# A depthwise convolution regrouped in PSUM, an expert decode on paired elements, and a gather ring of four

## The chip, the cores and the metric

The kernel runs on one core of a Trainium2 chip. The metric is the device time of one execution in microseconds (us). TensorE (PE) multiplies matrices, VectorE (DVE), ScalarE (ACT) and GpSimd (POOL) do elementwise work, and SyncE (SP) issues most of the DMAs. Each engine executes its own instructions in the order in which the program holds them, and waits on semaphores for the others.

## The reference, cut to what matters

Three parts of a long chain of layers matter here.

```python
# layer A: a causal depthwise convolution with 31 taps over 1536 channels, then LayerNorm and SiLU
h = a * sigmoid(gl)
h = conv(h, conv_w) + conv_b               # 12 tiles of 128 channels, 512 positions
y_mix = silu(layer_norm(h, g, b))          # then times silu(gate), then @ w_out

# peer_ffn, routing: per token and head the best 16 of 16 x 16 pair sums of two key lists
v1, i1 = top_k(s[:, :, 0], 16); v2, i2 = top_k(s[:, :, 1], 16)
top_s, pos = top_k(v1[..., :, None] + v2[..., None, :], 16)
idx = (i1 * 128 + i2) at pos; g = softmax(top_s)

# peer_ffn, experts: 16384 experts, 128 of them (8 heads x 16) chosen for each of 512 tokens
a = einsum('thkd,td->thk', u[idx], x); w = gelu(a) * g
out = einsum('thk,thkd->td', w, v[idx])
```

## The kernel before

Activations lie transposed, features on partitions and 512 tokens along the free axis. Float32 products are made of three matmuls (lines 164 to 166): each operand is split into a high part (a cast on ACT, `whi`, line 158) and a low part (a subtraction, `wlo`, line 159, on DVE or POOL by the argument `lo`).

The program is written stage by stage. A scheduler then orders the instructions of each engine by its own timeline, and tile pools with a fixed number of buffers bound how far it can run ahead: the next user of a buffer waits until its last reader is done.

**Layer A (`layer_a`, the first 400 us).** DVE makes eleven of the twelve convolution tiles: 31 multiply-adds (line 602, `cacc`) for each, a step of one tile followed by a step of its neighbour in the group `CGR`. The groups are (0,1), (3,4), (5,6), (7,8,9), (10,11). Two accumulators of a group lie in two PSUM banks; the third of (7,8,9), tile 9, lies in SBUF (tag `cva`). Tile 2 is made by ACT and POOL. Meanwhile PE makes the keys, values and attention of the memory (`mem_kv`, `mem_attn`, whose low parts `ak`, `av` and maxima `mmx` are made on DVE) and the gates. When the convolution is done, statistics are made (`cst` on PE, a chain on POOL), and broadcast as `Mb` and `Rb` in PSUM. Then for each tile: subtract the mean (line 607, DVE), multiply by `Rb` (four tiles on DVE, line 614; eight on POOL, line 616, from the SBUF copy `Rs`), scale and tanh on ACT, two products on DVE (lines 621 and 623), and the split into `y..h` and `y..l` (low parts of odd tiles on POOL, of even ones on DVE, line 187). The output projection on PE takes the y tiles in order, with weights split on ACT and DVE.

**Routing (`route`, to about 2010 us).** For tokens 384 to 511 (block t = 3) the 128 chosen experts of each token are fetched as rows: `gathered` issues an indirect DMA on POOL (line 1189; 128 rows of 8 KB, a u row and a v row) into the tile `grow`, DVE makes the dot product (line 1192) and adds the weighted v row to `pacc` (line 1199). `grow` has two buffers: gather n is issued when the addition of gather n - 2 is done. For the other 384 tokens all experts are computed densely. PE makes `u_tile` (24 matmuls of 384 columns each); 103 of the 128 tiles are spilled to DRAM (`a_spill`). `decode` turns positions into expert numbers on DVE by comparing with `tabs` (a table of 3 x 16 starts, copied out to 128 columns) and adding up steps; `dw` holds the steps copied out to 2048 columns by ACT. `gate_tiles` makes one-hot tiles on DVE (`oh`, `og`) which PE multiplies (`gp`, line 1319) into a table of gates, written to DRAM.

**Experts (`experts`, about 2010 to 2652 us).** For each of 128 expert tiles: load `vraw` (four buffers), split it (`vhi` on ACT, `vlo` on DVE), load the spilled `as` (four buffers) or make a fresh u tile (`pa`, every fifth, 25 in all), multiply by the gates `G`, split (`wh`, `wl`), and 18 matmuls of 512 columns into six PSUM banks (`po`). The rest of the 128 gathers lies between.

Of the kernel before, what the change touches and what calls it, by code (L numbers as in the profile page):

```python
# [17 lines left out]
OP = mybir.AluOpType  # L18
# [29 lines left out]
MLO = 6  # L48
CGR = (0, 1), (3, 4), (5, 6), (7, 8, 9), (10, 11)
NWARM = 8  # L50
# [8 lines left out]
class Body:  # L59
# [249 lines left out]
    def run(self):  # L309
        nc = self.nc  # L310
        self.vecs = self.const.tile([128, NVEC], F32, name="vecs")
        self.ident = self.const.tile([128, 128], F32, name="ident")
        self.ones = self.const.tile([128, 128], F32, name="ones")
        self.mhalf = self.const.tile([128, 8], F32, name="mhalf")
        nc.vector.memset(self.ones, 1.0)
        nc.vector.memset(self.mhalf, -0.5)
        self.hg_scale = self.const.tile([128, 1], F32, name="hg_scale")
        self.banks(alias=dict(o="s", Rb="cv", Mb="cv"), mm=(0, 1, 2), pt=(3, 4), s=(5,), cv=(6, 7))
        self.right = ExitStack()
        self.bk = self.right_pool("bk")  # L320
        if True:
            with self.phase("A", cva=1, slot=12, pcv=4, scr=2, asc=2, app=2, sq=2, accq=1, accs=1, back=4):
                with self.tc.tile_pool(name="mem", bufs=1) as self.mem:
                    self.layer_a()
            if self.stop == "a":
                self.right.close()
                return
            self.banks(mm=(0, 1), s=(2, 5), pt=(3, 4), o=(6, 7))
            with self.phase("B", slot=14, scr=4, asc=2, app=2, logit=3, alibi=2):
                self.layer_b()  # L330
        with self.right:
            self.banks(alias=dict(Rb="s", Mb="o"), mm=(0, 1, 2, 5), pt=(3, 4), s=(6,), o=(7,))
            with self.phase("B3", slot=24, scr=3, sq=2, accq=1, accs=1, back=2, raq=1, rsq=2, rtq=4, pp=3):
                self.b_out()
                self.ybp.close()
            if self.stop == "b":
                return
            self.banks(mm=(0, 1), s=(2, 5), pt=(3,), o=(4,), hx=(6, 7))
            self.early_c2 = ExitStack()
            self.c_mix()  # L340
            if self.stop == "c1":
                self.early_c2.close()
                return
            with self.early_c2, self.phase("C2", slot=24, scr=4, sq=2, accq=1):
                self.c_out()
            if self.stop == "c2":
                return
            self.pe = self.right_pool("pe")
            self.route_experts()
# [187 lines left out]
    def layer_a(self):  # L537
# [55 lines left out]
        for js in CGR:  # L593
            accs = [self.scr("cacc", tag="cva") if u == 2 else self.bank("cv", "cacc") for u in range(len(js))]
            for t in range(CK):
# [10 lines left out]
        for c in cs:  # L606
            nc.vector.tensor_tensor(c, c, Mb, op=OP.subtract)
        Rs = self.scr("Rs", tag="accs")
        nc.scalar.copy(Rs, Rb)
        for j in range(12):  # L610
            c = cs[j]
            n = self.scr("cn", tag=("asc", "app")[j % 2])
            if j % 3 == 0:
                nc.vector.tensor_tensor(n, c, Rb, op=OP.mult)
            else:
                nc.gpsimd.tensor_tensor(n, c, Rs, op=OP.mult)
            c = n
# [5 lines left out]
            nc.vector.scalar_tensor_tensor(y, c, 0.25, y, op0=OP.mult, op1=OP.mult)  # L623
            Y[4 + j] = self.split(y, f"y{j}", hi="s", lo="vg"[j % 2], x=2 <= j < 10, tag="slot" if j < 2 else "pcv")
        self.new_x()
# [558 lines left out]
    def gathered(self):  # L1184

        nc, n = self.nc, self.ng
        self.ng += 1
        gt = self.pe.tile([128, 2 * D], F32, name="grow", tag="grow", bufs=2)
        nc.gpsimd.indirect_dma_start(out=gt, out_offset=None, in_=self.i["peer_uv"],  # L1189
# [20 lines left out]
    def decode(self, vv, ii, tabs):  # L1210
# [11 lines left out]
        for h in range(8):  # L1222
            self.top16(c[:, h], ts[:, h], pos[:, h], 50)
        g = pool.tile([128, 8, 16], F32, name="g", tag="g", bufs=2)
        nc.vector.tensor_tensor(g, ts, ts[:, :, 0:1].to_broadcast([128, 8, 16]), op=OP.subtract)
# [7 lines left out]
        nc.vector.tensor_tensor(di[:, :, :, 1:16], ii[:, :, :, 1:16], ii[:, :, :, 0:15], op=OP.subtract)  # L1233
        dw = []
        for n in range(2):
            w = pool.tile([128, 16, 8, 16], BF16, name="dw", tag="dw", bufs=1)
            nc.scalar.copy(w, di[:, :, n].rearrange("p h r -> p r h").unsqueeze(3).to_broadcast([128, 16, 8, 16]))
            dw.append(w.rearrange("p r h k -> p r (h k)"))
        pf = pool.tile([128, 128], BF16, name="pf", tag="pf")
        nc.vector.tensor_copy(pf, pos.rearrange("p h k -> p (h k)"))  # L1240
        wide = [128, 16, 128]
        i1 = pool.tile([128, 128], F32, name="i1", tag="i1", bufs=2)
# [3 lines left out]
        def steps(src, n):  # L1246
            ge = pool.tile(wide, BF16, name="ge", tag="ge")
            nc.vector.tensor_tensor(ge, src.unsqueeze(1).to_broadcast(wide), tabs[:, n], op=OP.is_ge)
            return ge

        def total(ge, w, out):

            pr = pool.tile(wide, BF16, name="pr", tag="pr")
            nc.vector.tensor_tensor(pr, ge, w, op=OP.mult)
            n = 8
            while n:
                two = pr.rearrange("p (r two) x -> p r two x", two=2)
                o = out.unsqueeze(1) if n == 1 else pool.tile([128, n, 128], BF16, name="tree", tag=f"tree{n}")
                nc.vector.tensor_tensor(o, two[:, :, 0], two[:, :, 1], op=OP.add)
                pr, n = o, n // 2  # L1260

        ge = steps(pf, 0)
        total(ge, dw[0], i1)
        total(ge, tabs[:, 1], st)
        nc.vector.tensor_tensor(st, pf, st, op=OP.subtract)
# [3 lines left out]
    def route_tables(self):  # L1269
# [4 lines left out]
        nc.scalar.dma_start(starts, self.i["starts"])  # L1274
        tabs = pool.tile([128, 3, 16, 128], BF16, name="tabs")
        for n in range(3):
            nc.scalar.copy(tabs[:, n], starts[:, n].unsqueeze(2).to_broadcast([128, 16, 128]))
        rows = pool.tile([128, 128], F32, name="iota")
# [5 lines left out]
    def gate_tiles(self, t, ps):  # L1284
# [7 lines left out]
        nc.scalar.copy(g1, gs)  # L1292
        r = pool.tile([128, 128], F32, name="gr", tag="gr", bufs=2)
        nc.vector.tensor_tensor(r, gs, g1, op=OP.subtract)
# [30 lines left out]
    def experts(self):  # L1325
# [5 lines left out]
        for n in range(128):  # L1331
            e = n
            if n % 8 == 0:
                G = pool.tile([128, 24, 8, 16], F32, name="G", tag="G", bufs=2)
                nc.sync.dma_start(G.rearrange("p b n t -> p b (n t)"),
                                  self.gd[:, :, n * 16:n * 16 + 128].rearrange("b p c -> p b c"))
            vraw = pool.tile([128, D], F32, name="vraw", tag="vraw", bufs=4)
            nc.sync.dma_start(vraw, tab[e * 128:(e + 1) * 128, D:])
            vh, vl = self.split_w(vraw, "v", "v", 3, pool)
            vh, vl = (t.rearrange("p a b -> p (a b)") for t in (vh, vl))  # L1340
            if not self.fresh(e):
                a = pool.tile([128, ND], F32, name="as", tag="as", bufs=4)
                nc.sync.dma_start(a, self.ad[:, pre])
# [146 lines left out]
```

## Time and profile before

| | us |
|---|---|
| median of 3 runs (range) | 2709.32 (2707.19 to 2710.68) |
| the profiled execution, its own time | 2716.38 |
| span in the trace | 2714.4 |
| PE busy | 2621.4 (97% of the span) |
| DVE busy | 2077.2 (77%) |
| ACT busy / POOL busy | 1247.2 / 952.8 |

The busy time of PE is modelled: a matmul counts until its result is out, while the next one already streams. So the idle time of PE, the waits that end in it and the granted clock say more than the 97%. DVE, ACT and POOL rows overlap a little at their ends; the distance from start to start is what an instruction costs.

### The profile page before, as it was taken

The numbers are of one execution on the slowest core, as the hardware profiler recorded it, in microseconds if no ns is written. First come the engines' busy times: TensorE is split into PE (matmuls) and PEld (weight loads), VectorE is DVE, ScalarE is ACT, GpSimd is POOL, SyncE is SP. The second block draws the span as 40 slices with busy tenths as digits, with TensorE's granted clock in tenths as the row PEclk, the third lists the DMA queues.
The fourth block names the chain that finished last, engine by engine and source line by source line (L and its number), as shares of the span: only waits on it lengthen the run. The fifth ranks groups of instructions, "written<-read, shape, count | busy, mean of one in ns | idle before, by whom it ended". The sixth has DMA issues, their size and how long they took to land.

```text
span 2714.4 us, 40123 instructions
## 1 busy us (share of the span) xinstructions
PE 2621.4 (97%) x14581; PEld 2284.0 (84%) x14581; DVE 2077.2 (77%) x3926; ACT 1247.2 (46%) x2173; POOL 952.8 (35%) x654
## 2 busy tenths in 40 slices
PE   9989989999999999999999999999999999999998
PEld 7777879788889977788899999898898888888876
DVE  8999876695557678763679999888877877787765
ACT  4535554455545444333443555555543443343333
POOL 5965654332206555553431123223311121111201
PEclk9999999999999999999999999999999999999999
DMA  5233355223246311225733788788899899999952
GB/s 183 86 109 116 125 163 172 87 82 98 82 152 209 109 55 55 66 87 167 217 96 115 239 291 309 289 324 294 316 369 340 304 330 332 335 327 338 338 191 93
DMA packets 211958, 542.20 MB, mean 200 GB/s; under 512 B 18224, under 2 KB 105904, under 8 KB 192304
## 3 DMA queue, kind: packets, MB, share of 16 engines
q1 hardware_dynamic: 183488, 395.30, 44.3%
q0 software_dynamic: 18432, 134.23, 13.3%
q10 hardware_dynamic: 9840, 10.12, 1.2%
q8 instruction: 114, 1.87, 0.3%
q14 instruction: 84, 0.69, 0.1%
HBM read 468.99 MB, written 70.58 MB: 199 GB/s over the span
## 4 chain that ended last, share of the span: by engine, by line
PE 50%; DMA 14%; DVE 12%; issue 4%; ACT 2%; POOL 1%; SPq 0%; DVEq 0%; POOLq 0%; ACTq 0%
DMA grow<-peer_uv,pidx 9%; PE mm L164 9%; PE mm L165 9%; PE mm L166 8%; PE po L166 4%; PE po L164 4%; PE po L165 4%; DMA as<-a_spill 3%; PE out L164 2%; PE out L165 2%; PE out L166 2%; DVE pacc L1199 1%; DVE wlo L159 1%; DVE og L1312 1%; DVE hK L917 1%
## 5 line engine op out<-in xcount | busy, mean ns | idle before, releaser
L1189 POOL DMA_INDIRECT grow<-peer_uv,pidx x128 | 236.8, 1850 | 914.8 <-DVE pacc L1199 751.8
L158 ACT CAST whi<-wraw 128x1024 fp32r<-128x1024 f32 x360 | 377.6, 1050 | 383.9 <-PE mm L165 194.4
L159 POOL TENSOR_TENSOR wlo<-wraw,whi 128x1024 fp32r<-128x1024 f32 x157 | 380.7, 2427 | 419.6 <-ACT whi L158 360.9
L164 PE MATMUL po<-vhi,wh 128*128 128x512 f32 x768 | 297.1, 392 | 4.0 <-ACT wh L1351 4.0
L165 PE MATMUL po<-vlo,wh 128*128 128x512 f32 x768 | 299.0, 391 | 0.0
L159 DVE TENSOR_TENSOR wlo<-wraw,whi 128x1024 fp32r<-128x1024 f32 x203 | 260.1, 1283 | 48.2 <-ACT whi L158 45.4
L166 PE MATMUL po<-vhi,wl 128*128 128x512 f32 x768 | 273.6, 393 | 3.2 <-DVE wl L1352 3.2
L602 DVE SCALAR_TENSOR_TENSOR cacc<-h,vecs,cacc 128x512 f32<-128x512 f32 x319 | 240.0, 815 | 0.4
L1192 DVE SCALAR_TENSOR_TENSOR grow<-grow,hrow 128x1024 f32<-128x1024 f32 x128 | 156.6, 1223 | 101.2 <-DMA grow<-peer_uv,pidx 101.2
L166 PEld LDWEIGHTS po<-vhi,wl 128*128 128x128 f32 x768 | 143.9, 188 | 36.7 <-DVE wl L1352 6.6
L164 PEld LDWEIGHTS po<-vhi,wh 128*128 128x128 f32 x768 | 144.0, 188 | 34.2 <-ACT wh L1351 4.6
L165 PEld LDWEIGHTS po<-vlo,wh 128*128 128x128 f32 x768 | 144.3, 188 | 27.9
L159 DVE TENSOR_TENSOR vlo<-vraw,vhi 128x1024 fp32r<-128x1024 f32 x128 | 156.4, 1222 | 11.7 <-ACT vhi L158 11.6
L1199 DVE SCALAR_TENSOR_TENSOR pacc<-grow,pwc,pacc 128x1024 f32<-128x1024 f32 x127 | 162.8, 1282 | 2.3 <-ACT pwc L1195 1.8
L1194 ACT ACTIVATE pwc<-pac 128x1 f32<-128x1 f32 x128 | 25.9, 202 | 275.7 <-DVE grow L1192 275.6
L158 ACT CAST vhi<-vraw 128x1024 fp32r<-128x1024 f32 x128 | 133.8, 1046 | 34.4 <-DMA vraw<-peer_uv 18.1
L1351 ACT CAST wh<-as 128x384 fp32r<-128x384 f32 x103 | 52.6, 510 | 145.8 <-PE po L165 133.3
L1321 ACT COPY stage<-gp 128x512 f32<-128x512 f32 x96 | 96.9, 1101 | 44.9 <-PE gp L1319 44.9
L164 PE MATMUL mm<-X0h,whi 128*128 128x512 f32 (+2 forms) x294 | 109.8, 378 | 6.0 <-ACT pa L1181 2.6
L1319 PE MATMUL gp<-og,oh 128*128 128x128 bf16 x1152 | 95.7, 227 | 17.4 <-DVE og L1312 17.0
L165 PE MATMUL mm<-X2l,whi 128*128 128x512 f32 (+2 forms) x294 | 106.6, 363 | 0.6 <-DVE X2l L529 0.6
L164 PE MATMUL mm<-X2h,whi 128*128 128x512 f32 (+2 forms) x294 | 105.6, 359 | 1.4 <-ACT X2h L528 1.4
(984 smaller groups left out, 7762.8 us busy)
## 6 DMA issues: line engine op xcount, KB each, us to landing
wraw<-peer_uT SPq DMA_DIRECT2D x128, 512.0 KB, 5.7
vraw<-peer_uv SPq DMA_DIRECT2D x128, 512.0 KB, 7.0
gates<-stage SPq DMA_DIRECT2D x24, 1024.0 KB, 6.7
G<-gates SPq DMA_DIRECT2D x16, 1536.0 KB, 14.5
wraw<-a_w_in SPq DMA_DIRECT2D x43, 512.0 KB, 3.5
wraw<-c_w_in SPq DMA_DIRECT2D x42, 512.0 KB, 3.5
wraw<-b_w_in SPq DMA_DIRECT2D x39, 512.0 KB, 3.6
a_spill<-pa SPq DMA_DIRECT2D x103, 192.0 KB, 5.5
```

The costliest lines, as they stand in the source:

```text
L158: nc.scalar.copy(h, src)
L159: (nc.gpsimd if lo == "g" else nc.vector).tensor_tensor(l, src, h, op=OP.subtract)
L164: nc.tensor.matmul(ps, w[0], x[0], start=start, stop=False)
L165: nc.tensor.matmul(ps, w[0], x[1], start=False, stop=False)
L166: nc.tensor.matmul(ps, w[1], x[0], start=False, stop=stop)
L602: nc.vector.scalar_tensor_tensor(a if t < CK - 1 else cs[j], src, wc, a, op0=OP.mult, op1=OP.add)
L1189: nc.gpsimd.indirect_dma_start(out=gt, out_offset=None, in_=self.i["peer_uv"], in_offset=bass.IndirectOffsetOnAxis(ap=self.idx[:, n:n + 1] ...
L1192: nc.vector.scalar_tensor_tensor(gt[:, :D], gt[:, :D], 1.0, self.hrow, op0=OP.mult, op1=OP.mult, accum_out=ac)
L1199: nc.vector.scalar_tensor_tensor(self.acc, gt[:, D:], wc, self.acc, op0=OP.mult, op1=OP.add)
L1319: nc.tensor.matmul(gp[:, u * 128:(u + 1) * 128], oh2[:, bu[0], :, bu[1]], o[:, bu[0], :, bu[1]], start=n == 0, stop=n == 2)
L1321: nc.scalar.copy(stage[:, :, h + q:h + q + 4].rearrange("p n t -> p t n"), gp.rearrange("p (t n) -> p t n", t=4))
L1351: nc.scalar.copy(wh, a)
```

## The change

Three edits.

- **Convolution.** The groups are (0,1), (3,4), (5,6), (7,8), (9,10), (11). All accumulators lie in PSUM, and the pool `cva` is gone. In the LayerNorm behind it all twelve multiplications by `Rb` are on DVE, the copy `Rs` is gone, and the low parts of all y tiles are made on DVE.
- **Decode.** Tables and steps are kept twice instead of 128 times (`tabs` 3 x 16 x 2, `d2` 2 x 8 x 32), and the wide DVE operations read them with repeated patterns whose inner run is a pair. The counts of elements are the same. ACT makes one copy of 512 elements for each block instead of two of 2048.
- **Buffers.** `grow` has four instead of two, `vraw` and `as` three instead of four, `g` and `gr` one instead of two.

```diff
-CGR = (0, 1), (3, 4), (5, 6), (7, 8, 9), (10, 11)
+CGR = (0, 1), (3, 4), (5, 6), (7, 8), (9, 10), (11,)
-            accs = [self.scr("cacc", tag="cva") if u == 2 else self.bank("cv", "cacc") for u in range(len(js))]
+            accs = [self.bank("cv", "cacc") for _ in js]
-        Rs = self.scr("Rs", tag="accs")
-        nc.scalar.copy(Rs, Rb)
-            if j % 3 == 0:
-                nc.vector.tensor_tensor(n, c, Rb, op=OP.mult)
-            else:
-                nc.gpsimd.tensor_tensor(n, c, Rs, op=OP.mult)
+            nc.vector.tensor_tensor(n, c, Rb, op=OP.mult)
-            Y[4 + j] = self.split(y, f"y{j}", hi="s", lo="vg"[j % 2], ...)
+            Y[4 + j] = self.split(y, f"y{j}", hi="s", lo="v", ...)
-        gt = self.pe.tile([128, 2 * D], F32, name="grow", tag="grow", bufs=2)
+        gt = self.pe.tile([128, 2 * D], F32, name="grow", tag="grow", bufs=4)
-        dw = []
-        for n in range(2):
-            w = pool.tile([128, 16, 8, 16], BF16, name="dw", tag="dw", bufs=1)
-            nc.scalar.copy(w, di[:, :, n].rearrange("p h r -> p r h").unsqueeze(3).to_broadcast([128, 16, 8, 16]))
-            dw.append(w.rearrange("p r h k -> p r (h k)"))
+        d2 = pool.tile([128, 2, 8, 32], BF16, name="d2", tag="d2")
+        nc.scalar.copy(d2.rearrange("p n h (r u) -> p n h r u", u=2),
+                       di.rearrange("p h n r -> p n h r").unsqueeze(4).to_broadcast([128, 2, 8, 16, 2]))
+        dw = [d2[:, n].unsqueeze(2).to_broadcast([128, 8, 8, 32]) for n in range(2)]
-        wide = [128, 16, 128]
+        wide = [128, 64, 16, 2]
-            nc.vector.tensor_tensor(ge, src.unsqueeze(1).to_broadcast(wide), tabs[:, n], op=OP.is_ge)
+            nc.vector.tensor_tensor(ge, src.rearrange("p (x u) -> p x u", u=2).unsqueeze(2).to_broadcast(wide),
+                                    tabs[:, n].unsqueeze(1).to_broadcast(wide), op=OP.is_ge)
...
-            vraw = pool.tile([128, D], F32, name="vraw", tag="vraw", bufs=4)
+            vraw = pool.tile([128, D], F32, name="vraw", tag="vraw", bufs=3)
-                a = pool.tile([128, ND], F32, name="as", tag="as", bufs=4)
+                a = pool.tile([128, ND], F32, name="as", tag="as", bufs=3)
```

The order of the instructions changes in layer A, in the routing and in the experts; between them (layer B and the mixer) DVE's rows stand as before.

**The convolution on DVE**, in the middle of layer A. A row is one step of one tile; the number behind `h` names the tile (`h9` is tile 9, `cacc_3000` its accumulator in SBUF). Before:

```order
L602 SCALAR_TENSOR_TENSOR cacc_3000<-h9_922,vecs_70,cacc_3000 128x512
L602 SCALAR_TENSOR_TENSOR cacc_2998<-h7_788,vecs_70,cacc_2998 128x512
L602 SCALAR_TENSOR_TENSOR cacc_2923<-h6_721,vecs_70,cacc_2923 128x512
L602 SCALAR_TENSOR_TENSOR cacc_3000<-h9_922,vecs_70,cacc_3000 128x512
L602 SCALAR_TENSOR_TENSOR cacc_2998<-h7_788,vecs_70,cacc_2998 128x512
```

And now:

```order
L600 TENSOR_SCALAR cacc_2999<-h8_855,vecs_70 128x512
L602 SCALAR_TENSOR_TENSOR cacc_2998<-h7_788,vecs_70,cacc_2998 128x512
L602 SCALAR_TENSOR_TENSOR cacc_2999<-h8_855,vecs_70,cacc_2999 128x512
L602 SCALAR_TENSOR_TENSOR cacc_2998<-h7_788,vecs_70,cacc_2998 128x512
L602 SCALAR_TENSOR_TENSOR cacc_2999<-h8_855,vecs_70,cacc_2999 128x512
```

Before, three tiles take turns, and every third step is that of tile 9; now two do, and tile 11 is alone at the end.

**The experts on DVE**, around the 21st expert's `vlo` (`grow,pac` is the dot product of a gather, `pacc` its addition). Before:

```order
L159 TENSOR_TENSOR vlo<-vraw,vhi 128x1024
L1192 SCALAR_TENSOR_TENSOR grow,pac<-grow,hrow 128x1024
L1347 TENSOR_TENSOR as<-as,G 128x384 x2
L1199 SCALAR_TENSOR_TENSOR pacc<-grow,pwc,pacc 128x1024
L1352 TENSOR_TENSOR wl<-pa,wh 128x384
L159 TENSOR_TENSOR vlo<-vraw,vhi 128x1024
L1347 TENSOR_TENSOR as<-as,G 128x384
L159 TENSOR_TENSOR wlo<-wraw,whi 128x1024
L1352 TENSOR_TENSOR wl<-as,wh 128x384
L1192 SCALAR_TENSOR_TENSOR grow,pac<-grow,hrow 128x1024
```

And now:

```order
L1187 SCALAR_TENSOR_TENSOR grow,pac<-grow,hrow 128x1024
L1345 TENSOR_TENSOR as<-as,G 128x384
L1350 TENSOR_TENSOR wl<-as,wh 128x384
L1194 SCALAR_TENSOR_TENSOR pacc<-grow,pwc,pacc 128x1024
L1187 SCALAR_TENSOR_TENSOR grow,pac<-grow,hrow 128x1024 x2
L1350 TENSOR_TENSOR wl<-as,wh 128x384
L1194 SCALAR_TENSOR_TENSOR pacc<-grow,pwc,pacc 128x1024
L159 TENSOR_TENSOR vlo<-vraw,vhi 128x1024
L1194 SCALAR_TENSOR_TENSOR pacc<-grow,pwc,pacc 128x1024
L159 TENSOR_TENSOR vlo<-vraw,vhi 128x1024
L1187 SCALAR_TENSOR_TENSOR grow,pac<-grow,hrow 128x1024
L1345 TENSOR_TENSOR as<-as,G 128x384
```

The gathers stand closer together and earlier. Counted over DVE's whole order: ahead of the first `vlo` there are 55 dot products before and 76 now (and 175 `wlo` before, 179 now), and the 128th stands behind 118 `vlo` before and behind 46 now.

## Rows read from the trace of the kernel before

**Rows 1.** Windows, layer A: length, busy us (count) PE PEld DVE ACT POOL, PEclk, DMA share, GB/s.

```profile
100.00:200.00 100.00, 91.65 (x485) 79.68 (x484) 100.00 (x124) 39.33 (x59) 75.53 (x42) 0.95 0.34 101
...
300.00:400.00 100.00, 89.62 (x459) 76.95 (x458) 76.85 (x85) 53.22 (x85) 53.25 (x41) 0.91 0.44 140
```

**Rows 2.** Waits of PE from 100 to 400 us: total us, times, longest.

```profile
PE mm L164 <- ACT mk L414: 5.2, 1, 5.2
PE msc L164 <- ACT mp L446: 5.1, 2, 3.5
PE out L164 <- ACT whi L158: 3.8, 2, 2.2
PE cst L290 <- DVE h L602: 3.6, 1, 3.6
PE out L166 <- DVE wlo L159: 3.0, 1, 3.0
```

**Rows 3.** Windows of line 602 on DVE alone: length, busy (count), clock, DMA share, GB/s.

```profile
130.00:218.00 88.00, 81.49 (x87) 0.94 0.32 99
218.00:302.00 84.00, 70.80 (x103) 1.00 0.41 132
```

**Rows 4.** Timeline of DVE, POOL, ACT: start us, length, what, count, [idle before].

```profile
25.04 6.30 DVE L602 SCALAR_TENSOR_TENSOR cacc<-h,vecs,cacc 128x512 f32<-128x512 f32 x8
...
168.02 5.68 DVE L602 SCALAR_TENSOR_TENSOR cacc<-h,vecs,cacc 128x512 f32<-128x512 f32 x4
...
288.54 6.66 DVE L602 SCALAR_TENSOR_TENSOR cacc<-h,vecs,cacc 128x512 f32<-128x512 f32 x10
...
167.71 2.65 POOL L159 TENSOR_TENSOR wlo<-wraw,whi 128x1024 fp32r<-128x1024 f32 x1 [2.21 <-ACT whi L158]
...
161.29 0.37 ACT L414 COPY mk<-mm 128x256 f32<-128x256 f32 x1 [6.66 <-DVE ak L223]
```

**Rows 5.** Groups of DVE, then POOL, from 331 to 390 us (busy, mean ns | idle before).

```profile
L621 DVE SCALAR_TENSOR_TENSOR cn<-th,cn 128x512 f32<-128x512 f32 x12 | 15.0, 1275 | 1.6 <-ACT th L620 1.6
L623 DVE SCALAR_TENSOR_TENSOR gb<-cn,gb 128x512 f32<-128x512 f32 x12 | 12.6, 1064 | 3.3 <-DMA gb<-a_gates 3.2
...
L616 POOL TENSOR_TENSOR cn<-h,Rs 128x512 f32<-128x512 f32 x8 | 10.3, 1291 | 14.4 <-DVE gb L623 6.5 <-issue 4.4 <-ACT Rs L609 3.5
```

**Rows 6.** Waits from 1523 to 2011 us, of DVE and of PE.

```profile
DVE grow L1192 <- DMA grow<-peer_uv,pidx: 57.3, 22, 6.2
...
PE gp L1319 <- DVE og L1312: 17.0, 9, 3.5
```

**Rows 7.** Windows of the routing and the experts, columns as in rows 1.

```profile
1523.00:2011.00 488.00, 468.00 (x3329) 441.63 (x3328) 420.79 (x683) 258.91 (x407) 139.83 (x57) 0.98 0.87 309
2011.00:2233.00 222.00, 220.49 (x1014) 187.07 (x1013) 163.97 (x215) 89.01 (x155) 31.89 (x23) 1.00 0.95 333
2000.00:2050.00 50.00, 48.49 (x249) 44.24 (x248) 33.49 (x43) 22.26 (x35) 5.97 (x4) 1.00 1.06 382
```

**Rows 8.** Groups of DVE, 1500 us to the end (busy, mean ns | idle before).

```profile
L1199 DVE SCALAR_TENSOR_TENSOR pacc<-grow,pwc,pacc 128x1024 f32<-128x1024 f32 x127 | 162.8, 1282 | 2.3 <-ACT pwc L1195 1.8
L1192 DVE SCALAR_TENSOR_TENSOR grow<-grow,hrow 128x1024 f32<-128x1024 f32 x128 | 156.6, 1223 | 101.2 <-DMA grow<-peer_uv,pidx 101.2
...
L1308 DVE TENSOR_TENSOR oh<-keys,k 128x1024 bf16<-128x1024 bf16 x48 | 33.1, 690 | 0.0
...
```

**Rows 9.** The page, part 3: the gathers' DMA queue: packets, MB, share of 16 engines.

```profile
q0 software_dynamic: 18432, 134.23, 13.3%
```

**Rows 10.** Timeline of PE: two starts 72 u-tile matmuls apart, two 13 expert matmuls apart.

```profile
1480.48 0.33 PE L164 MATMUL mm<-X2h,whi 128*128 128x384 f32 x1
...
1492.96 0.33 PE L164 MATMUL mm<-X2h,whi 128*128 128x384 f32 x1
...
2649.11 0.39 PE L164 MATMUL po<-vhi,wh 128*128 128x512 f32 x1
...
2652.06 0.39 PE L166 MATMUL po<-vhi,wl 128*128 128x512 f32 x1
```

More of the change, by code (lines that the diff above doesn't have):

```diff
@@ L321, in run @@
         if True:
-            with self.phase("A", cva=1, slot=12, pcv=4, scr=2, asc=2, app=2, sq=2, accq=1, accs=1, back=4):
+            with self.phase("A", slot=12, pcv=4, scr=2, asc=2, app=2, sq=2, accq=1, accs=1, back=4):
                 with self.tc.tile_pool(name="mem", bufs=1) as self.mem:
@@ L623, in layer_a @@
             nc.vector.scalar_tensor_tensor(y, c, 0.25, y, op0=OP.mult, op1=OP.mult)
-            Y[4 + j] = self.split(y, f"y{j}", hi="s", lo="vg"[j % 2], x=2 <= j < 10, tag="slot" if j < 2 else "pcv")
+            Y[4 + j] = self.split(y, f"y{j}", hi="s", lo="v", x=2 <= j < 10, tag="slot" if j < 2 else "pcv")
         self.new_x()
@@ L1223, in decode @@
             self.top16(c[:, h], ts[:, h], pos[:, h], 50)
-        g = pool.tile([128, 8, 16], F32, name="g", tag="g", bufs=2)
+        g = pool.tile([128, 8, 16], F32, name="g", tag="g", bufs=1)
         nc.vector.tensor_tensor(g, ts, ts[:, :, 0:1].to_broadcast([128, 8, 16]), op=OP.subtract)
@@ L1253, in total @@
             pr = pool.tile(wide, BF16, name="pr", tag="pr")
-            nc.vector.tensor_tensor(pr, ge, w, op=OP.mult)
+            flat = lambda t: t.rearrange("p (h k) r u -> p h k (r u)", h=8)
+            nc.vector.tensor_tensor(flat(pr), flat(ge), w, op=OP.mult)
             n = 8
             while n:
-                two = pr.rearrange("p (r two) x -> p r two x", two=2)
-                o = out.unsqueeze(1) if n == 1 else pool.tile([128, n, 128], BF16, name="tree", tag=f"tree{n}")
-                nc.vector.tensor_tensor(o, two[:, :, 0], two[:, :, 1], op=OP.add)
+                two = pr.rearrange("p x (r two) u -> p x r two u", two=2)
+                if n == 1:
+                    o = out.rearrange("p (x r u) -> p x r u", r=1, u=2)
+                else:
+                    o = pool.tile([128, 64, n, 2], BF16, name="tree", tag=f"tree{n}")
+                nc.vector.tensor_tensor(o, two[:, :, :, 0], two[:, :, :, 1], op=OP.add)
                 pr, n = o, n // 2
@@ L1263, in decode @@
         total(ge, dw[0], i1)
-        total(ge, tabs[:, 1], st)
+        total(ge, tabs[:, 1].rearrange("p r u -> p (r u)").unsqueeze(1).unsqueeze(1).to_broadcast([128, 8, 8, 32]), st)
         nc.vector.tensor_tensor(st, pf, st, op=OP.subtract)
@@ L1274, in route_tables @@
         nc.scalar.dma_start(starts, self.i["starts"])
-        tabs = pool.tile([128, 3, 16, 128], BF16, name="tabs")
-        for n in range(3):
-            nc.scalar.copy(tabs[:, n], starts[:, n].unsqueeze(2).to_broadcast([128, 16, 128]))
+        tabs = pool.tile([128, 3, 16, 2], BF16, name="tabs")
+        nc.scalar.copy(tabs, starts.unsqueeze(3).to_broadcast([128, 3, 16, 2]))
         rows = pool.tile([128, 128], F32, name="iota")
@@ L1292, in gate_tiles @@
         nc.scalar.copy(g1, gs)
-        r = pool.tile([128, 128], F32, name="gr", tag="gr", bufs=2)
+        r = pool.tile([128, 128], F32, name="gr", tag="gr", bufs=1)
         nc.vector.tensor_tensor(r, gs, g1, op=OP.subtract)
```

## The prediction

> **What bounds the kernel now.** Read the windows first, not the 97% of PE in the page. Where PE streams without a break, 72 matmuls of u tiles start in 12.48 us and 13 of the experts in 2.95 us [rows 10]: 0.173 and 0.227 us each, 4.16 us for a u tile (24) and 4.08 us for an expert (18). Nothing in the change touches the number of matmuls, so it can only win back what PE loses, or make it lose more. Three places lose.
>
> In layer A, PE idles 8.3 us of the window 100 to 200 and 10.4 us of 300 to 400 [rows 1], and the granted clock is 0.95 and 0.91 of full speed there, which is the lower of its two levels for about 10 and 18 us, or some 14 us of work. DVE is 100% busy beside it. The waits of PE name ACT more often than DVE [rows 2], but ACT only passes it on: the copy `mk` stood 6.66 us behind DVE's `ak` [rows 4], and `ak` stands in DVE's queue behind steps of the convolution. The listed waits sum to 20.7 us.
>
> In the routing, from the first gather to the first `vlo` (1523 to 2011 us), DVE is busy for 421 of 488 us and stands 57.3 us in front of gathered rows [rows 6, 7]; PE waits 17.0 us for the one-hot tiles `og` queued behind that. In the experts PE idles 1.5 of the first 222 us [rows 7], with the DMA engines busy 0.95 of the time at 333 GB/s. That is the stage to fear: two resources are close to full there.
>
> **The change, part by part.**
>
> *Convolution.* From 130 to 218 us, while tile 9 is in turn with its accumulator in SBUF, 87 steps took 81.5 us, 0.937 each; from 218 to 302 us 103 took 70.8 us, 0.687 each [rows 3]. The difference is 87 x 0.25 = 21.7 us of DVE. One run shows how: four steps take 5.68 us, with a POOL subtraction of 2.65 us beside them, where ten take 6.66 us elsewhere [rows 4]. With the accumulator in PSUM these steps read one tile in SBUF like the others, so I take all 21.7 us away. Against that, tile 11 now stands alone, each step on the sum of the one before it: eight such steps took 6.30 us, 0.79 each, against 0.66 in turns [rows 4], 31 x 0.13 = +4.0 us. In the LayerNorm 14 operations move from POOL to DVE. POOL's `cn` goes: eight of 1.29 us [rows 5]. DVE gets 14 x about 0.6, +8.4 us, but its products 621 and 623, 24 of them, took 27.6 us beside POOL, where an unhindered step takes 0.69 [rows 3, 5], 16.6 us; 11 us of hindrance has no more cause. So -2.6 us. DVE gains 21.7 - 4.0 + 2.6 = 20 us in a stage in which it is late.
> For PE the lateness is 20.7 us of waits and 14 us of slow clock, 35 in all. It does not all go: DVE also serves the y tiles, and the weights' `wlo` now stand behind 14 more operations (+8.4 us against the 11). Bounds: 6 us (only `cst` and a little) and 30 us (nearly all). I take half, **-18 us**. The new order leaves DVE's rows in layer B and the mixer as they were: nothing there.
>
> *Decode.* Counts of elements stay. `oh` already reads pairs, 1024 elements in 0.69 us [rows 8], the price of the wide operations now; I take 0. If the adding trees, whose pairs are not adjacent, cost twice, 12 of them with 1920 elements each, 1.3 us at that rate, would add 16 us to DVE, most of it in the routing. ACT loses 2048-wide copies that nobody waits for: 0.
>
> *Four gather buffers, routing.* DVE's new order has 76 dot products ahead of the first `vlo` instead of 55, and 179 `wlo` instead of 175. By starts a gather costs DVE some 1.15 + 1.20 us (0.08 under the means of [rows 8]): 21 x 2.35 = 49 us, and the four `wlo` some 5 us, by the same rule. They fill the 57.3 us of waits, if four buffers make these vanish; 8 us of wait I leave. The stretch goes from 488 to 488 - 57 + 49 + 5 + 8 = 493 us, +5 (bounds -8, +15). PE has four u tiles less to do behind it: 4 x 4.16 = **-17 us**. POOL's queue holds only gathers here, each behind a later `pacc`, so nothing else waits for them.
>
> *Experts.* All of the 52 gathers left now stand ahead of the 47th `vlo`. Those 46 experts and 13 u tiles give PE 46 x 4.08 + 13 x 4.16 = 242 us of work. What has to land by then: 52 x 1.05 MB (134.23 / 128 [rows 9]), 59 tiles of 128x1024 f32 (0.52 MB), 38 spilled tiles (0.20 MB), 6 tables G (1.57 MB), in all 102 MB; about 7 MB of that are there at the start (two gathers, a table, a few weights), so 95 MB. At 382 GB/s, which the DMA engines did over 50 us [rows 7], that is 249 us, 7 over PE's work; at 333 / 0.95 = 350 GB/s it is 271 us, 29 over it. I take **+10**, since the stretch at 382 is the one in which the engines were pressed. Three buffers of `vraw` and `as` cost something only in this stretch, where it is the same wait. The other 82 experts have no gathers left, and PE lost little there: 0.
>
> Sum: -18 + 5 - 17 + 10 = **-20 us**. On the profiled execution (2716.4 us, of it span 2714.4) that is 2696; on the median of the runs, 7 us below it, 2689.
>
> The Trainium skill, "DMA: Bandwidth & Descriptors", Specifications, speaks against this: it gives about 358 GB/s as the limit of one core's HBM traffic. The trace passes it: 382 GB/s for 50 us [rows 7]. By the page the 95 MB would take an estimated 265 us, 13 us more than I took, and the time would be about 2702 us.
>
> **The rivals.**
>
> *The gathers are pulled together until DMA bounds the experts, and it is slower.* DVE takes its queue in order, so a gather that is late holds `vlo` and `wl`, and PE behind them. For it: 0.95 busy before, with 0.57 gathers for each expert, and now 1.1 for each of the first 46. Against it: 382 GB/s. If the stretch runs at the 333 GB/s that it had, 95 MB take 285 us, 43 over PE; with +12 instead of +5 in the routing and only 10 us won in layer A this is -10 + 12 - 17 + 43 = +28, 2737 us. It decides from where DMA and routing give back 35 us or more: below some 345 GB/s. The page's limit lies above that point.
>
> *Layer A gives nothing.* DVE is earlier, but PE's order has the same weights behind the LayerNorm, and idles at another place: -4 instead of -18, 2703 us, or 2710 with the DMA between. That is within 0.2% of before, or near it.
>
> *More than half comes back.* -30 in layer A (the slow clock goes with the waits), -8 in the routing, +0 in the experts: -30 - 8 - 17 = -55, 2654 us; half of that extra, 2670.
>
> *The pairs cost double*: +16 on DVE in the routing, about 2705 us.
>
> **How the numbers follow.** 0.2% is 5.4 us, about what a measurement of this kernel can tell from no change. The forecast, 2689 with a range of its own of 2676 to 2702: 0.45. More comes back: 0.17. Layer A gives nothing: 0.13. DMA bounds: 0.21. Pairs: 0.04. The forecast, the larger gain and half of the pairs are faster, 0.64; layer A's case and the rest of the pairs are the same, 0.14 with a little of the DMA case; slower 0.22. The range for 8 in 10 leaves out the ends of the larger gain and of the DMA case: 2660 to 2727.
>
> **What would show it.** Right: line 602 from 130 to 218 us costs under 0.72 us a step everywhere, PE's waits from 100 to 400 us fall to about 10 us and the clock there rises; DVE's wait for `grow` up to the first `vlo` falls from 57 to about 10 us with 76 gathers done, and that `vlo` starts within 10 us of 2011 less what layer A won; the 47th `vlo` comes 245 to 260 us later, and the last 82 experts run at 4.1 to 4.2 us. Wrong: DVE waits of over 40 us for `grow` and `as` ahead of the 47th `vlo` with DMA at a share of 1.0 (the first rival); PE waits in layer A unchanged; `ge`, `pr` or `tree` longer than before.

## The result and the profile after

| | before | after |
|---|---|---|
| median of the runs, us (range, runs) | 2710.0 (2707.19 to 2713.88, 4) | 2738.93 (2734.98 to 2744.09, 4) |
| ratio, 95% interval | | 1.0107 (1.0085 to 1.0129) |
| span in the trace, us | 2714.4 | 2733.2 |

The change makes the kernel 1.1% slower: the sign was forecast wrong, and the time lies 12 us above the range. The page's slices (40 of 68 us each) show where. The first place is a dip of PE and of its clock at slice 30; from there PE stays at 8 for some four slices while the DMA row stands at 9.

```profile
PE   9999999999999999999999999999858888999998
PEclk9999999999999999999999999999979999999999
DMA  5244464132355211236435999999999998666642
```

**Layer A won more than forecast.** Windows of layer A, columns as in [rows 1]: PE is idle 0 and 1.3 us where it was 8.3 and 10.4, and the clock rises with it, to 1.00 and 0.97. The listed waits of PE from 100 to 400 us (20.7 us in [rows 2]) are 1.8 us.

```profile
100.00:200.00 100.00, 100.00 (x544) 87.06 (x543) 99.27 (x154) 47.40 (x78) 81.89 (x48) 1.00 0.38 116
300.00:400.00 100.00, 98.67 (x553) 86.37 (x554) 73.55 (x94) 55.99 (x83) 35.24 (x28) 0.97 0.54 172
```

```profile
PE out L164 <- ACT whi L158: 1.1, 2, 0.9
PE cst L290 <- DVE h L602: 0.7, 1, 0.7
```

Line 602 alone on DVE: 74.32/110 = 0.676 us a step, and 0.687 later, against 0.937 and 0.687 in [rows 3].

```profile
130.00:218.00 88.00, 74.32 (x110) 1.00 0.40 125
218.00:302.00 84.00, 61.81 (x90) 1.00 0.45 144
```

**Routing, first experts, the rest** (the first gather's dot product starts at 1503 us, the first `vlo` at 2007, the first matmul of the 47th expert at 2289). The counterparts of [rows 7]:

```profile
1503.00:2007.00 504.00, 467.08 (x3392) 446.06 (x3390) 469.10 (x719) 263.30 (x453) 161.20 (x77) 0.97 0.96 354
2007.00:2289.00 282.00, 246.55 (x1067) 203.62 (x1068) 235.62 (x308) 105.56 (x218) 69.17 (x48) 0.95 0.97 350
2289.00:2670.00 381.00, 378.22 (x1695) 315.96 (x1694) 191.16 (x249) 131.43 (x181) 0.00 (x0) 1.00 0.61 189
```

In the routing DVE is busier than before (469 of 504 us against 421 of 488), and its wait for `grow` is gone (57.3 us in [rows 6]):

```profile
DVE wlo L159 <- ACT whi L158: 12.6, 14, 2.3
DVE pa L1345 <- DMA G<-gates: 11.8, 1, 11.8
...
DVE grow L1187 <- DMA grow<-peer_uv,pidx: 3.7, 4, 1.8
```

Yet PE stands still for 32 us ahead of the first expert. The window, PE's longest wait from 1900 to 2030 us, and what SP and DVE did there (start, duration, engine and line; in brackets the idle time before and what ended it):

```profile
1975.00:2007.00 32.00, 0.00 (x0) 0.00 (x0) 16.65 (x21) 6.62 (x15) 9.19 (x6) 0.54 1.01 376
```

```profile
PE po L164 <- ACT vhi L158: 32.5, 1, 32.5
```

```profile
1982.43 0.38 SPq L1333 DMA_DIRECT2D G<-gates  x1
1982.87 19.02 SPq L1336 DMA_DIRECT2D vraw<-peer_uv  x2
2001.93 0.43 SPq L1341 DMA_DIRECT2D as<-a_spill  x1
```

```profile
1991.77 1.28 DVE L1194 SCALAR_TENSOR_TENSOR pacc<-grow,pwc,pacc 128x1024 f32<-128x1024 f32 x1 [0.60 <-ACT pwc L1190]
2004.83 1.03 DVE L1345 TENSOR_TENSOR pa<-pa,G 128x384 f32<-128x384 f32 x2 [11.78 <-DMA G<-gates]
```

The last u tile is through at 1975; the table `G` is asked for at 1982 and lands at 2005; the issue of the first `vraw`, straight behind that of `G`, holds SP for 18.5 of the 19.02 us (the second takes 0.43); and the DMA engines move 376 GB/s at a share of 1.01 all the while. In the 282 us behind it they stay at 0.97. In before `G` lands 12 us after its issue, not 22, and 209 matmuls of u tiles cover the way. The transfers of that stage (issues, size, median us from issue to landing), 48 gathers among them:

```profile
DMA packets 40378, 97.40 MB, mean 350 GB/s; under 512 B 2373, under 2 KB 27086, under 8 KB 34218
...
vraw<-peer_uv SPq DMA_DIRECT2D x46, 512.0 KB, 7.9
G<-gates SPq DMA_DIRECT2D x6, 1536.0 KB, 14.8
as<-a_spill SPq DMA_DIRECT2D x36, 192.0 KB, 8.0
...
grow<-peer_uv,pidx POOLq DMA_INDIRECT x48, 8.9
```

**One account for all kernels.** The distance from one matmul's start to the next, less the median distance for its number of columns (0.173 us for 384, 0.227 for 512, as in [rows 10]), summed over a stage, is what PE lost there, slow clock included. The totals of before and after differ by 18.8 us, and so do the spans. In us, from the traces:

| kernel | layer A, to 400 | 400 to first dot product | routing, to first `po` | first 46 experts | rest | median of runs |
|---|---|---|---|---|---|---|
| before | 47.5 | 70.0 | 48.5 | 2.3 | 19.4 | 2710 |
| after | 17.0 | 69.7 | 51.8 | 52.7 | 15.4 | 2739 |
| e1_conv_alone | 20.5 | 69.7 | 45.1 | 2.3 | 16.7 | 2683 |
| e2_ring_two | 19.0 | 70.2 | 47.3 | 2.4 | 17.7 | 2686 |
| e3_no_conv | 49.6 | 70.1 | 52.3 | 60.5 | 15.0 | 2772 |
| e4_paced | 17.5 | 67.6 | 12.8 | 33.1 | 53.3 | 2709 |
| e5_paced_deep | 20.5 | 69.7 | 16.4 | 12.5 | 28.7 | 2684 |
| e6_two_shallow | 21.5 | 70.7 | 51.0 | 9.4 | 29.7 | 2699 |
| e7_cover | 18.9 | 70.8 | 69.6 | 42.4 | 13.7 | 2746 |
| e8_spread | 17.0 | 70.6 | 52.3 | 18.1 | 34.1 | 2723 |
| e9_front | 19.0 | 69.4 | 52.4 | 65.9 | 15.1 | 2737 |
| e10_half_bytes | 16.8 | 72.6 | 48.0 | 10.2 | 14.9 | 2688 |
| e11_no_add | 17.5 | 69.5 | 52.9 | 58.1 | 15.4 | 2743 |
| e12_paced_free | 21.1 | 70.1 | 16.4 | 12.5 | 9.8 | 2656 |

Layer A gives 30 us, the first 46 experts take 50, and the hole of 32 us adds only 3 to what the routing lost before: there PE waited in many small pieces, now in one. (One of e8_spread's ten executions took 9082.92 us, a slow one; it is left out of the ratio, and the median is the same to 0.1 us without it.)

### The profile page after: what moved, and what is told of

Read it like the earlier page. It is cut to its first block, busy times and chain, and to the rows that moved or that the text cites. A ratio compares the mean times of both kernels' runs of the same rounds, so it can differ in the third digit from the quotient of the medians.

```text
span 2733.2 us, 40066 instructions
## 1 busy us (share of the span) xinstructions
PE 2617.5 (96%) x14581; PEld 2282.5 (84%) x14581; DVE 2061.1 (75%) x3940; ACT 1229.7 (45%) x2166; POOL 931.9 (34%) x640
## 4 chain that ended last, share of the span: by engine, by line
PE 68%; DVE 6%; DMA 5%; ACT 3%; issue 2%; POOL 1%; SPq 0%; ACTq 0%; DVEq 0%; POOLq 0%
PE mm L164 13%; PE mm L165 12%; PE mm L166 12%; PE po L164 6%; PE po L165 5%; PE po L166 5%; PE gp L1317 2%; DMA vraw<-peer_uv 2%; PE out L164 2%; PE out L165 2%; PE out L166 2%; DVE hK L912 1%; DVE pacc L1194 1%; DMA G<-gates 1%; DVE grow L1187 1%
## 5 line engine op out<-in xcount | busy, mean ns | idle before, releaser
L164 PE MATMUL po<-vhi,wh 128*128 128x512 f32 x768 | 269.5, 403 | 60.7 <-ACT vhi L158 59.1
L166 PE MATMUL po<-vhi,wl 128*128 128x512 f32 x768 | 290.9, 393 | 0.0
L267 POOL TENSOR_TENSOR sq<-sq 128x256 f32<-128x256 f32 (+1 forms) x51 | 67.2, 1318 | 448.9 <-ACT sq L260 448.3
L602 DVE SCALAR_TENSOR_TENSOR cacc<-h,vecs,cacc 128x512 f32<-128x512 f32 x319 | 218.0, 749 | 0.6
L1349 ACT CAST wh<-as 128x384 fp32r<-128x384 f32 x103 | 52.9, 513 | 229.8 <-PE po L165 222.8
L1345 DVE TENSOR_TENSOR as<-as,G 128x384 f32<-128x384 f32 x103 | 56.9, 557 | 85.3 <-DMA as<-a_spill 85.1
L166 PE MATMUL mm<-X0h,wlo 128*128 128x512 f32 (+2 forms) x294 | 106.4, 362 | 3.3 <-DVE wlo L159 3.2
L165 PE MATMUL mm<-X0l,whi 128*128 128x512 f32 (+2 forms) x294 | 106.6, 363 | 0.7 <-DVE X0l L529 0.7
```

The source lines that it names most:

```text
L164: nc.tensor.matmul(ps, w[0], x[0], start=start, stop=False)
L165: nc.tensor.matmul(ps, w[0], x[1], start=False, stop=False)
L166: nc.tensor.matmul(ps, w[1], x[0], start=False, stop=stop)
L267: nc.gpsimd.tensor_tensor(self.accq[:, c], self.accq[:, c], sq[:, c], op=OP.add)
L602: nc.vector.scalar_tensor_tensor(a if t < CK - 1 else cs[j], src, wc, a, op0=OP.mult, op1=OP.add)
L1345: nc.vector.tensor_tensor(a.rearrange("p (b t) -> p b t", t=16), a.rearrange("p (b t) -> p b t", t=16), G[:, :, e % 8], op=OP.mult)
```

## The experiments

**Which of the three edits loses.** Two kernels take edits out of after, one puts the convolution alone into before.

```diff
 e1_conv_alone (to before): CGR, accs, Rs, L611 and lo="v" as in after
 e3_no_conv (to after):     the same lines as in before
 e2_ring_two (to after):
-  name="grow", tag="grow", bufs=4      name="vraw", tag="vraw", bufs=3      name="as", tag="as", bufs=3
+  name="grow", tag="grow", bufs=2      name="vraw", tag="vraw", bufs=4      name="as", tag="as", bufs=4
```

> The kernel before with the convolution and LayerNorm of after alone (groups, PSUM accumulators, line 614 and the low parts on DVE); decode and buffers as before. Before is 2710 us. Between the profiles of before and after the first dot product of a gather came 31 us earlier (1534 to 1503). Theory A, the layer's gain is real and stays to the end: 2710 - 31 = about 2679. Theory B, it is given back behind layer A, where the weights' DMAs or DVE are late next: 2700 to 2710.

> After with two buffers for grow and four for vraw and as, as before: so the new convolution and the new decode together, and no deeper ring. Theory A, the loss sits in the buffers and the order that they bring: about 2679, as with the convolution alone, DVE's wait for grow in the routing back near 57 us and 209 to 221 matmuls of u tiles left behind the last gate matmul. Theory B, reading pairs costs DVE time: 16 us more than the convolution alone, 2695. Theory C, the earlier start of the routing is itself what starves the experts: 2720 or more.

> After with the convolution and LayerNorm of before: the new decode, four buffers for grow and three for vraw and as. Theory A, the ring of four loses 79 us at the boundary and in the first 47 experts (PE's idle time over its streaming pitch from 1900 to 2300 us was 18 us in before and 89 in after, plus the lower clock) and wins some 20 in the routing, whatever comes ahead: 2710 + 60 = about 2770. Theory B, the loss comes of the routing starting earlier: 2710 to 2720.

Measured: e1_conv_alone 2682.71 (0.9904 of before, 0.9873 to 0.9934), e2_ring_two 2686.26 (0.9921, 0.9895 to 0.9948), e3_no_conv 2772.1 (1.0225, 1.019 to 1.0261). Theory A three times. The convolution is worth 27 us and keeps them; the decode in pairs adds 3.6 us or nothing (the intervals overlap); buffers and the order that they bring cost some 53 us on top of it, and 62 without it (decode included). By its time alone e2_ring_two lies between theory A (2679) and theory B (2695); that the wide operations cost what they did (below) decides for A. `g` and `gr` stay at one buffer in it, so they are no part of the loss. The stages of e1_conv_alone from the first dot product on, for comparison with the windows above: DVE is less busy, and in the first 46 experts PE is busy throughout.

```profile
1506.00:1992.00 486.00, 467.69 (x3326) 441.67 (x3325) 421.46 (x669) 258.36 (x408) 131.35 (x55) 0.98 0.89 313
1992.00:2219.00 227.00, 227.00 (x1043) 192.44 (x1042) 171.76 (x224) 92.07 (x163) 32.69 (x26) 1.00 0.94 331
```

**Is the hole what costs?** After has 48 matmuls of u tiles behind the last gate matmul, before has 209. e7_cover holds seven u tiles back.

```diff
 (self.gp: the latest gate matmul)
+            with self.tc.issue_after(self.gp.ins) if n >= 96 else nullcontext():
-            nc.sync.dma_start(self.ad[:, n], self.u_tile(e))
+                nc.sync.dma_start(self.ad[:, n], self.u_tile(e))
```

> After with one thing held: the matmuls of the last seven spilled u tiles stand behind the last gate matmul (240 matmuls of 384 columns behind it instead of 48); gathers, buffers and the rest of the order as in after (76 gathers ahead of the first vlo, 127 ahead of the 47th). Theory A, the hole of 32 us ahead of the first expert is the missing cover of the trip gates - G and vraw - vhi: it goes, and 2739 - 32 = about 2707. Theory B, the trip is long because the gathers fill the DMA engines, and PE is late either way (it idles in the routing instead, or the trip grows): 2725 to 2739.

Measured: 2746.15 (1.0123, 1.0095 to 1.0151). Theory A falls; theory B is right in kind, 7 us past its range. Most of the idle time moved ahead of the last gate matmul, where DVE is busy without a break and PE has nothing left that it may do (first line); behind it, ahead of the first expert, PE still stands for 11.6 of 60 us (second line), and the routing loses 69.6 us in all:

```profile
1920.00:1957.00 37.00, 21.42 (x174) 17.86 (x173) 36.93 (x57) 16.77 (x28) 10.80 (x7) 0.50 0.80 274
1957.00:2017.00 60.00, 48.43 (x262) 47.75 (x261) 37.81 (x45) 22.29 (x43) 13.21 (x9) 0.89 1.02 373
```

So the time of the last gate matmul is set by DVE, which (as in after) has done 68 gathers by the last one-hot tile where before had done 51. The loss in the experts (42.4) is there without the hole.

**Where the gathers stand, and how many buffers there are.** e8_spread and e4_paced keep after's buffers and move gathers, by holding a dot product: it is queued on DVE behind all that the program has written for DVE ahead of it; e5_paced_deep gives `vraw` and `as` their fourth buffer back (`grow` has three, to make room); e6_two_shallow is e2_ring_two with three buffers of `vraw` and `as`.

```diff
 e8_spread:
-NGAT = 48
+NGAT = 76
+        if pin:
+            self.tc.keep_in_program_order(dot)
 (in experts)
-                self.gathered()
+                self.gathered(pin=True)
 e4_paced: the same with NGAT = 64, and
 (behind the routing of block t = 3)
+                for _ in range(7):
+                    self.gathered()
 (in gate_tiles, behind each group of og)
+                self.gathered(pin=True)
 (behind the last u tiles)
-            if n * NGAT // NPRE < (n + 1) * NGAT // NPRE:
-                self.gathered()
+            if n >= 92 and self.ng < NGAT:
+                self.gathered(pin=True)
```

> After with the same buffers (four grow, three vraw and as), but the dot products held to places in the program: seven free ones, one behind each of the 48 groups of og, five behind the last u tiles, one for every second expert. In DVE's order 62 gathers stand ahead of the first vlo (76 in after), 86 ahead of the 47th (127), and 216 matmuls of u tiles stand behind the last gate matmul (48 in after, 209 in before). Theory A, the place of the gathers is the loss (they take the cover of the trip gates - G - vraw and then fill the DMA engines): PE's hole of 32 us ahead of the first expert and most of the 45 us in the first 47 experts go, 2739 - 32 - 40 = about 2667. Theory B, three buffers of vraw and as are the loss in the experts: the hole goes, the stretch stays, about 2707. Theory C, the ring of four as such (its traffic) is the loss: about 2739.

> After with the 52 gathers that are left at the first vlo spread over all 128 experts (their dot products held to places in the program, 18 instead of 51 ahead of the 47th vlo); routing and buffers as in after. Theory A, the first 47 experts are slow because 51 gathers fill the DMA engines there (274 us for PE's 242): the stretch gets 30 us shorter, 2739 - 30 = about 2709. Theory B, three buffers of vraw and as lose in all experts that have gathers beside them (49 us in the paced kernel at 0.52 each, so some 39 at 0.41 against the 25 of after): about 2753.

> After with two buffers for grow, and vraw and as left at three: the run with two and four (2686) less a buffer each; no instruction is held. Theory A, three buffers lose wherever gathers run beside them (70 of them along 113 experts here, 0.6 for each): about 2686 + 50 = 2736, DVE's wait for as over 150 us in the experts. Theory B, the loss in the paced kernel came of the held dot products: about 2686.

> The paced kernel (e4_paced) with four buffers each for vraw and as, and three for grow to make room. The paced kernel lost its gain in the experts: 677 us from first to last vlo against 628 with the convolution alone, with DVE waiting 172 us for as (45 there) while the DMA engines were busy only 0.81 to 0.84 of the time. Theory A, three buffers of vraw and as are too few where gathers run beside them: DVE's wait for as falls to about 45 us and the time to about 2709 - 45 = 2664. Theory B, the dot products held in program order are the loss: about 2709 again, with the waits as they were.

Measured: e4_paced 2709.33 (1.0003, 0.998 to 1.0025), e8_spread 2722.54 (1.0036, 1.0022 to 1.005), e6_two_shallow 2698.58 (0.9943, 0.9924 to 0.9963), e5_paced_deep 2683.61 (0.9896, 0.987 to 0.9922). The 2709 of e4_paced is theory B's number; the other three lie between their theories. Two causes show, and neither alone fits all numbers. Placement: with 18 instead of 52 gathers in the first 46 experts they lose 18 us instead of 53 (e8_spread), and with one gather for each group of gates the routing loses 13 instead of 52 (e4_paced). Buffers: with three of `vraw` and `as` and held dot products, the other experts lose where gathers run beside them (53 and 34 us in e4_paced and e8_spread, 15 in after, which has none left there), and DVE waits for `as`. Its largest wait in the experts, of e4_paced and of e5_paced_deep:

```profile
DVE as L1349 <- DMA as<-a_spill: 171.7, 61, 9.5
```

```profile
DVE as L1349 <- DMA as<-a_spill: 85.0, 38, 10.0
```

The step from three to four buffers is worth 26 us in the paced kernel, which also lost a `grow` buffer. Without any holding (e6_two_shallow against e2_ring_two) it is 12 us by the medians, but the intervals of the two ratios overlap, and DVE's wait for `as` is 53.4 against 45.1 us; theory A of e6_two_shallow had asked for 50 us and a wait of over 150. So what three buffers cost by themselves isn't clear of noise. The rest of the paced kernel's loss in the experts was the holding itself, as the last run shows.

**Bytes or DVE?** In the first 46 experts of after both were nearly full: the DMA engines at 0.97, DVE at 235.62/282 = 84%, with PE's waits naming ACT's `vhi` (2030 to 2285 us) and DVE not waiting for gathered rows at all (its waits for `as` in the stage sum to 3.5 us).

```profile
PE po L164 <- ACT vhi L158: 26.6, 11, 5.5
```

```profile
DVE as L1345 <- DMA as<-a_spill: 3.5, 3, 1.8
```

e9_front holds the late gathers where after has them; the other two each take one cost away from it.

```diff
 e9_front (to e8_spread):
-            while self.ng < NGAT + (n + 1) * (128 - NGAT) // 128:
+            while self.ng < NGAT + min((n + 1) * (128 - NGAT) // 45, 128 - NGAT):
 e10_half_bytes (to e9_front):
+        if n >= 76:
+            out, rows = gt[:, :D], rows.rearrange("e (two d) -> (e two) d", two=2)
 (and the addition to pacc reads gt[:, :D] for these)
 e11_no_add (to e9_front): the addition to pacc
-        else:
+        elif n < 76:
```

> A control for the next two: after with the 52 late gathers held at the places that they have in after anyway (51 ahead of the 47th vlo), so that taking work out of them doesn't move them. Expected as after: 2735 to 2745, PE's idle time over its streaming pitch in the first 46 experts about 53 us (2 in before).

> The control, with the last 52 gathers reading 4 KB for each row instead of 8 KB (a row of half the length, and the same half used for the product and the addition, so the v half is left out and the result is not the reference's). DVE, ACT and POOL keep every instruction; the transfers of the first 46 experts shrink by 52 x 0.52 = 27 MB of about 95. Theory A, the DMA engines bound this stretch: 27 MB at the 350 GB/s of this stretch are 78 us of transfers, more than the 52 us lost, so nearly all comes back: 2690 to 2700. Theory B, DVE and the queues behind it bound it (DVE was busy 84% there, and waited for gathered rows not at all): 2735 again.

> The control, with the additions (pacc) of the last 52 gathers left out; their transfers, dot products and places stay, and the result lacks these rows. DVE has 51 x 1.20 = 61 us less to do in the first 46 experts, no DMA changes. Theory B, DVE bounds the stretch: most of the 52 us comes back, 2690 to 2700. Theory A, the DMA engines bound it: 2725 to 2740.

Measured: e9_front 2737.4 (1.0098, 1.0081 to 1.0115), e10_half_bytes 2688.08 (0.9914, 0.9894 to 0.9934), e11_no_add 2743.4 (1.0133, 1.0112 to 1.0153). The first 46 experts of the three in that order:

```profile
2010.00:2305.00 295.00, 248.58 (x1069) 205.24 (x1069) 235.72 (x309) 104.72 (x217) 69.15 (x48) 0.94 0.94 334
```

```profile
2006.00:2241.00 235.00, 231.05 (x1040) 194.00 (x1041) 212.72 (x284) 101.40 (x204) 65.78 (x44) 0.99 0.89 295
```

```profile
2009.00:2296.00 287.00, 244.16 (x1067) 202.91 (x1067) 175.38 (x258) 105.80 (x216) 55.31 (x48) 0.95 0.95 344
```

60 us less work on DVE (235.72 to 175.38) brings nothing; half of the bytes of 52 gathers, with every instruction kept, takes 60 us off the stage (47 against after's 282) and 49 off the kernel (the profiled run of e9_front is a long one, 13 us over its median). Leaving out the addition frees a `grow` buffer earlier, but the gathers kept their pace: 48 are issued from 2007 to 2285 us in after, e10_half_bytes and e11_no_add alike. The transfers bound the stage. That PE's waits name ACT and that DVE hardly waits for transfers does not speak against it. The transfers of `vraw` show the link: in these 278 us the median from issue to landing is 7.9 us in after, 8.6 in e11_no_add and 5.6 in e10_half_bytes:

```profile
vraw<-peer_uv SPq DMA_DIRECT2D x56, 512.0 KB, 5.6
```

One place in after shows it singly: behind an issue of `G`, SP needs 10 us for two issues of `vraw`, and an ACT `vhi` 21 us later waits for `vraw` (its bracket names the DMA), PE behind it.

```profile
2090.74 0.38 SPq L1333 DMA_DIRECT2D G<-gates  x1
2091.88 10.05 SPq L1336 DMA_DIRECT2D vraw<-peer_uv  x2
...
2112.73 6.34 SPq L1336 DMA_DIRECT2D vraw<-peer_uv  x3
```

```profile
2113.03 1.05 ACT L158 CAST vhi<-vraw 128x1024 fp32r<-128x1024 f32 x1 [0.90 <-DMA vraw<-peer_uv]
2116.40 1.05 ACT L158 CAST vhi<-vraw 128x1024 fp32r<-128x1024 f32 x1 [2.33 <-DMA vraw<-peer_uv]
```

**A version that beats both.** e12_paced_free is e5_paced_deep with the holding taken out of the experts; in the routing it stays.

```diff
 (in experts)
-                self.gathered(pin=True)
+                self.gathered()
```

> The paced kernel with three buffers for grow and four for vraw and as (e5_paced_deep), with the late gathers' dot products no longer held in program order; those in the routing stay held. PE's idle time over its pitch was 16 us in the routing (45 with the convolution alone) but 35 in the experts (13 there). Theory A, the holding itself cost the 22 us in the experts: about 2683 - 20 = 2663, the fastest. Theory B, three grow buffers make the free gathers run ahead and crowd the experts as in after: 2683 or more.

Measured: 2656.35 us (2651.75 to 2658.47), 0.9798 of before (0.9781 to 0.9816); 26 us under the convolution alone and 83 under after. Its stages from the first dot product on:

```profile
1507.00:1970.00 463.00, 459.97 (x3359) 438.19 (x3358) 428.94 (x668) 255.75 (x418) 98.69 (x61) 1.00 0.94 340
1970.00:2200.00 230.00, 223.08 (x1012) 188.75 (x1012) 179.16 (x235) 90.96 (x168) 32.19 (x28) 0.99 0.95 338
2200.00:2600.00 400.00, 397.67 (x1803) 333.69 (x1802) 286.84 (x378) 157.15 (x276) 47.34 (x38) 1.00 0.84 289
```

With a ring of three whose gathers keep nearly the pace that they had (60 ahead of the first `vlo` and 89 ahead of the 47th, 55 and 79 in e1_conv_alone) the routing loses 16 us instead of 45, and the experts 22 where they lost 19. Whether the third buffer or the places bring that gain isn't shown: no run has these places with a ring of two.

## Why the prediction was wrong

*Convolution: right mechanism, size too small.* The steps beside the tile in SBUF fell to 0.676 us (forecast: under 0.72). In the LayerNorm, lines 621 and 623, 27.6 us before, are 9.6 and 8.2 us, the 16.6 us that the prediction gave for 24 unhindered products and a little more:

```profile
L616 DVE SCALAR_TENSOR_TENSOR cn<-th,cn 128x512 f32<-128x512 f32 x12 | 9.6, 803 | 1.1 <-ACT th L615 1.1
L618 DVE SCALAR_TENSOR_TENSOR gb<-cn,gb 128x512 f32<-128x512 f32 x12 | 8.2, 691 | 6.0 <-DMA gb<-a_gates 6.0
```

DVE's gain came about as forecast: all 319 steps of line 602 took 240.0 us and take 218.0 now, where 21.7 less 4.0 were forecast. The term that was mis-sized is what this is worth to PE: -18 with bounds of 6 and 30; it measured -30.5 in the traces and -27 in e1_conv_alone. "I take half" had no row behind it: the waits (20.7 us to 1.8) and the slow clock went together. That DVE's lateness was the one cause of both is argued; which part the groups have in it and which the LayerNorm, no run separates.

*Decode: right.* The wide operations cost what they did (`pr` 1231 ns, before 1214; `tree` of 1024 elements 702, before 687), and e2_ring_two lies 3.6 us over e1_conv_alone.

*Routing: the steps that failed are the stretch, +5, and with it the gain "PE has four u tiles less to do behind it", -17.* The counts held (76 dot products ahead of the first `vlo`, a wait for `grow` of 3.7 us). But the stretch that was forecast to grow by 5 us, from the first gather's issue (1524 us before, 1496 now) to the first `vlo`, grew by 24, from 487 to 511, past its bound of 15. Of these, 10 us stand ahead of the last gate matmul: 18 of the 21 added gathers stand ahead of the last one-hot tile, and their 2.35 us each are DVE time on which the gates wait. The other 14 stand behind it, on the way gates - `G` - `vraw` - `vlo`, which took 27 us and takes 41: the prediction gave it no term. The u tiles done ahead (three by PE's own order, at the first `po`) were no gain; they left PE without work while the gates and `G` came late. The two terms sum to -12 in the prediction; the account shows +3.

*Experts: the step that failed is the rate.* 95 MB were forecast to land in 249 us at 382 GB/s. The trace shows 97 MB in the 278 us to the last gather, at 350 GB/s. The row of 382 came from 50 us with a share of 1.06 in which four gathers were issued; the stage as it is now, with 48 issued in 278 us, gave 350, the other bound in the prediction's own text (333 / 0.95). For one unit of share the two rows are the same rate, 382 / 1.06 = 360 and 350 / 0.97 = 361: what the prediction carried over 249 us was the share of those 50 us. The term was +10, with bounds of 7 and 29; PE lost 50 more than before. The 29 was short by 13 us because PE's own work was overrated, and by 7 because 97 MB landed and not 95: the 13 u tiles were counted in DVE's order, and by the trace PE had ten left in this stage, so 46 x 4.08 + 10 x 4.16 = 229 us of work against 97.4 / 0.350 = 278 us of transfers. What three buffers add in just this stretch was not tried with a ring of four; e10_half_bytes, which has both, loses 8 us more there than before (10.2 against 2.3), so without the bytes they cannot be worth more.

The Trainium skill, "DMA: Bandwidth & Descriptors", Specifications, cited with its 358 GB/s, would have put this term at +23 and the whole at 2702: nearer, and still on the wrong side. The 350 GB/s of the crowded stage lies 2% under its figure; the 50 us at 382 remain over it.

*The rival that was right* is the first, 2737 us, at a chance of 0.21: its 285 us for the stage measured 282. Its terms were off against each other: layer A 10 for 30, the routing -5 for +3, the experts 43 for 50. So that its number came within 2 us of the measured 2739 is in part luck. Its signature was put wrongly: DVE did not wait for `grow` or `as` (3.5 us in the stage); the lateness shows in how late `vraw` lands and in PE's wait for `vhi`. And its point of decision, 345 GB/s, was too low, since it stood on the same overrated work of PE: the stage ran at 350 and lost.

## What to carry to other kernels

Ask of a deeper prefetch ring not only which wait it removes but what the scheduler will pull forward into the time: here it filled an engine's idle time with work that another stage had done for nothing, ahead of the tiles that the next stage waits for, and crowded the DMA engines of a stage that had no slack. Cost the bytes of a stage at the lowest rate that the trace shows at a full share, not at the best one, and hold the pulled work to its old pace before judging the ring. Where two engines are both nearly full, take work from each in turn with the order held, since the engine that the waits name need not be the one that bounds.

## What the hardware showed that was not expected

An issue on SP can hold its whole queue. In the hole, one issue of `vraw` took 18.54 of the 19.02 us shown, where most take 0.33 to 0.43, and the rest of the queue (`as`, the next `G`) waited with it. Full engines alone are not the reason: in each of the fourteen traces, every issue on SP of over 3 us stands straight behind an issue of the table `G`, in before as well, whose first 46 experts lose only 2.3 us, and in after's last experts, where the DMA share is 0.61 (5.43 us at 2311). In before, at its first `G`:

```profile
1994.60 0.38 SPq L1335 DMA_DIRECT2D G<-gates  x1
1995.03 8.45 SPq L1338 DMA_DIRECT2D vraw<-peer_uv  x2
```

What in the transfer of `G` holds the queue, and why it was longest in the hole, stays open. And a DMA share near 1 is no fixed rate: 350 GB/s at 0.97 in after's first experts, 382 at 1.06 for 50 us of before, 376 at 1.01 in the hole. The first two are 361 and 360 GB/s for one unit of share, the third 372; why the share itself passes 1, and why it did so for just those 50 us, stays open.
